# A hybrid attention and expert layer: TensorE's order written out from the first score to the routing, and w2 loaded with two consecutive rows on a partition

## The chip, the cores and the metric

The kernel runs on one core of one Trainium2 chip. A core has a matmul engine (TensorE, PE in the rows; PEld is its loading of weights), VectorE (DVE), ScalarE (ACT), GpSimd (POOL) and SyncE (SP, which here only issues transfers), an on-chip memory of 128 partitions (SBUF) and accumulators for TensorE (PSUM). Each engine works through its own list of instructions in order, and semaphores tie the lists together. The metric is the device time of the whole program in microseconds (us).

## What is computed

One layer over 512 latent tokens of width 1024 and 256 context tokens, all values fp32. The latent rows form a grid of 8 x 64. The parts that the change touches are the attention, the routing and the experts:

```python
h = modulate(rmsnorm(x, norm1_g), sh1, sc1)
q, k, v, hy_in, cf_in = split(h @ w_in)                  # 8 heads of 64 for q, k, v
attn = neighbourhood_attention(q, k, v, k_ctx, v_ctx)    # 8 x 16 window, and all context keys, one softmax
x = x + g1 * (concat(attn, hyena(hy_in), conformer(cf_in)) @ w_out)
h2 = modulate(rmsnorm(x, norm2_g), sh2, sc2)
aff = softmax(h2 @ w_router)                             # 16 experts
gate, idx = top_k(aff.T, 64)                             # every expert takes its 64 best tokens
xe = h2[idx]
y = (silu(xe @ w1) * (xe @ w3)) @ w2                     # w1, w3: 16 x 1024 x 2048, w2: 16 x 2048 x 1024
x = x + g2 * scatter_add(y * gate)
return rmsnorm(x, final_norm_g)
```

The expert weights are 16 x 24 MB and are each read once.

## The kernel before, in words

**Stages.** The Hyena filters, the modulation, the projections and the Hyena and conformer groups come first (0 to some 265 us of the profile), then the attention with the output projection and the routing (to 418 us), then the 16 experts, two by two, and the final norm.

**Attention.** The work is 16 pairs of heads and token blocks: hp counts four pairs of heads, b four blocks of 128 tokens. `scores(hp, b)` (L924) makes, for the two heads of a pair, a score tile of 128 tokens by 512 keys (256 of the window, 256 of the context): one matmul for each head (L932), on the upper and the lower 64 rows of TensorE. Then for each head DVE adds the bias and takes the minimum (L940; scores are negated), ACT takes the exponential and its sum (L943), DVE the reciprocal and the product (L944, L945). `ptrans` (L949) turns a tile of probabilities with four 128 x 128 transposes into a PSUM buffer of the tag T, of which there are two, and copies it to SBUF, by turns on ACT and DVE (L103, L105). `av` (L957) multiplies the turned probabilities by the values, 8 matmuls of 64 columns (L963), and splits the result on ACT and DVE into a high and a low part.

**Work beside it.** `out_part` (L902) multiplies the Hyena and conformer groups by their half of w_out: 12 matmuls for each of four blocks and two halves n (three products of high and low parts, L548 to L550), then DVE and POOL add to x. `out_proj(n, b)` (L1006) does the same with the attention's half. `x_rows` (L1019) transposes rows of x for the router (L1022, the same two PSUM buffers), `route(b)` (L1026) makes the router's logits and softmax in four pieces (L1044, L1050, L1063). `adaln(3)` is the last part of the modulation (L423, L431).

**Who sets the order.** Every engine's instructions are put in order by a list scheduler that takes those with the best priority whose operands it reckons ready; the priorities follow the source. Inside `tc.manual_schedule(engines={PE})` the source alone sets the order of TensorE's instructions. Before, that holds for an early stage and for the experts, and not for the attention, whose source is the generator `attention()` (L970) with 13 steps called in a row and then a list of words (L1114 to L1137): p for out_proj, l for the first half of x_rows, r for the next piece of a route, q for a quarter of an out_proj, a for the next attention step, f for its end.

**Loads.** 22 buffers of 1 MB (U) hold weights. `load` (L157 on) puts loads into a fixed list; SP issues them (L162) as buffers become free (`free`, `free_only`, `pump`), at most 22 at a time. The experts' loads are the end of the list: per expert 16 of w1 and w3 (128 rows of 2048 columns, one row of 8 KB on a partition) and 8 of w2 (256 rows of 1024 columns, L265 to L267; the partition p gets the rows p and p + 128, 4 KB each).

**Experts.** For each pair of experts a gather (L1162 on) builds the tokens' rows from one-hot matrices (L1170 on DVE) with 128 x 128 matmuls (L1178), copied and modulated by DVE and ACT (L1072, L1070). Each expert multiplies them by w1 and w3 into four PSUM tiles pa (L1290, L1291), copies these to SBUF as au (four tiles, 64 rows of w1's product above 64 of w3's), turns each with four transposes (L1317; the piece of au is the weights of the matmul, ident the moving operand), applies silu and the product (L1319, L1320) into hT, and multiplies hT by w2 (L1330). The result is scattered back with one-hot matmuls (L1188) and DVE adds (L1191) during the next expert's products.

Of the kernel before, what the change touches and what calls it, by code (L numbers as in the profile page):

```python
# [19 lines left out]
S = 512  # L20
# [30 lines left out]
def hybrid_kernel(ctx: ExitStack, tc: tile.TileContext, a, out: bass.AP):  # L51
    nc = tc.nc
# [23 lines left out]
    def free(k=1, keep=0):  # L76
        used[0] -= k
        pump(keep)

    def free_only(k=1):  # L80
        used[0] -= k
# [30 lines left out]
    ident = c1[:, C1["id"]]  # L112
# [46 lines left out]
    def load(key, src, view=lambda t: t):  # L159
        def go():  # L160
            t = U("ld")
            nc.sync.dma_start(view(t), src)  # L162
            ready[key] = t
        loads.append(go)
# [96 lines left out]
    for e in range(E):  # L261
        for k in range(8):
            load(("w1", e, k), a["w1"][e, k * 128:(k + 1) * 128, :])
            load(("w3", e, k), a["w3"][e, k * 128:(k + 1) * 128, :])
        for j in range(8):  # L265
            load(("w2", e, j), a["w2"][e, j * 256:(j + 1) * 256].rearrange("(k p) n -> p k n", p=128),
                 lambda t: t.rearrange("p (k n) -> p k n", n=1024))  # L267


    def norm_rows(rows, junk, n, ss, name):  # L270
# [499 lines left out]
    def finish(*gens):  # L770
        for g in gens:
            for _ in g:
                pass
# [79 lines left out]
    parts = []  # L853
# [49 lines left out]
    def out_part(n):  # L903

        for b in range(4):
            ps = psA("pX")
            for k in range(4):
                mm3(ps, [v512(m[1])[:, k, 128 * b:128 * b + 128] for m in (mixh, mixl)],
                    [w[:, k] for w in wov[n, 1]], k == 0, k == 3)
                yield  # L910
            s = slice(n * 512, (n + 1) * 512)
            t = W("t")
            nc.vector.tensor_mul(t, ps, g1bc[:, s])
            nc.gpsimd.tensor_add(xblk(b)[:, s], xblk(b)[:, s], t)
# [52 lines left out]
        nc.scalar.activation(h, ps[:, 0:128], AF.Copy)  # L967
        nc.vector.tensor_sub(v512(mixl[0])[:, hp, c], ps[:, 0:128], h.bitcast(FT))

    def attention():  # L970
        ps = deque()
        steps = [(hp, b) for hp in range(2) for b in range(4)] + [(hp, b) for b in range(4) for hp in (2, 3)]
        parts = [out_part(0), out_part(1)]
        build_tm(1)
        fetch_bias(2)
        for i in range(len(steps) + 1):
            if i < len(steps):
                ps.append(scores(*steps[i]))
            for _ in range(4):
                if i < 4:  # L980
                    next(parts[0])
                elif 5 <= i < 9:
                    next(parts[1])
            if i == 8:
                finish(parts[1])
                free_only(4)
            if i >= 1:
                hp, b = steps[i - 1]
                av(b, hp, [ptrans(p) for p in ps.popleft()])
                if b == 3:  # L990

                    free((1, 2, 1, 3)[hp], PK[hp])
                    if hp < 2:
                        build_tm(hp + 2)
                    if hp == 0:
                        fetch_bias(3)
                    if hp == 1:
                        load_wo(0, 0, 2)
                        load_wo(1, 0, PK[4])
            if i == 3:  # L1000
                finish(parts[0])
                free_only(2)
                load_wo(1, 1, PK[5])
            yield

    def out_proj(n, b):  # L1006
        ps = psA("pX")
# [91 lines left out]

    xr = [take(("xr", 0)), take(("xr", 1))]  # L1100
    limit[0] = 99
    att = attention()
    ada3 = adaln(3)
    for i in range(13):
        next(att)
        if i >= 10:
            next(ada3)

    def steps(g, at):

        for i, _ in enumerate(g):
            for other in at.get(i, ()):
                next(other, None)

    def one(f, *args):
        f(*args)
        yield

    PE = {mybir.EngineType.PE}
    rt = [route(b) for b in range(4)]  # L1120
    left = lambda b: one(x_rows, b, 0)
    go = lambda *g: [next(i, None) for i in g]
    op = {(n, b): out_proj(n, b) for n in range(2) for b in range(4)}
    for w in "p00 l0 p10 a r0 a p11 p01 r0 l1 r1 r0 r1 a p02 p12 q13 r1 r2 q13 r1 r0 q03 l2 q03 a f p13 r2 p03 r2 l3 r3 r3 r2 r3 r3".split():
        if w == "a":
            go(att)
        elif w == "f":
            finish(att)
            free(2, 0)
        elif w[0] == "p":  # L1130
            finish(op[int(w[1]), int(w[2])])
        elif w[0] == "q":
            go(op[int(w[1]), int(w[2])])
        elif w[0] == "l":
            go(left(int(w[1])))
        elif w[0] == "r":
            go(rt[int(w[1])])  # L1137

    free(6, 0)
    finish(ada3)  # L1140
# [137 lines left out]
    for e in range(E):  # L1278
# [35 lines left out]
        for f in range(4):  # L1314
            p = psT("pT")
            for i in range(4):
                nc.tensor.transpose(p[:, i * 128:(i + 1) * 128], au[f][:, i * 128:(i + 1) * 128], ident)  # L1317
            pv = p.rearrange("p (i a n) -> p i a n", i=4, a=2)
            nc.scalar.activation(hT[:, 4 * f:4 * f + 4], pv[:, :, 0], AF.Silu)  # L1319
            nc.vector.tensor_mul(hT[:, 4 * f:4 * f + 4], hT[:, 4 * f:4 * f + 4], pv[:, :, 1])  # L1320
# [132 lines left out]
```

## Time and profile before

| what | value |
|---|---|
| median of 3 runs | 1370.36 us (1369.19 to 1371.82) |
| the profiled execution | 1374.3 us |
| its span, first to last instruction | 1372.4 us |
| PE busy | 1267.0 us, 92% of the span |
| DVE, ACT, POOL busy | 491.7, 213.8, 154.4 us |
| read from and written to HBM | 453.87 and 2.36 MB, 332 GB/s over the span |
| mean granted clock of TensorE | 0.955 |
| w1 and w3 matmuls (L1290, L1291) | 1024 each, 455.5 and 455.8 us |
| w2 matmuls (L1330) | 1024, 223.5 us |

The page of the profile lists each engine's busy time, cuts the span into 40 slices, and follows the chain that ended last back from the last instruction: at each step to what released it. The waits are told from semaphores: an engine was idle until an instruction of another engine or a transfer ended. A timeline row gives the start and the time of a run of like instructions on one engine. [...] The rows themselves stand below.

### The profile page before, as it was taken

The page shows a single profiled execution, that of the slowest core. Times are in us where ns is not written, and L with a number is a line of the kernel's source. Part 1 is how long each engine was busy: PE and PEld are TensorE (multiplying, and loading weights), DVE is VectorE, ACT ScalarE, POOL GpSimd, SP SyncE. Part 2 cuts the span into 40 slices and gives each one's busy share as a digit, 9 for nine tenths or more (in the row PEclk, how much of TensorE's full clock was granted, in tenths as well). Part 3 has the DMA queues.
Part 4 walks back from the last instruction along what each step waited for, and adds up shares of the span by engine and source line. Part 5 has one row for each costly group of instructions (what it writes and reads, how often), then busy time and mean ns, then how long its engine had stood idle before and what let it go on. Part 6 is the DMA issues. An engine that isn't in the chain of part 4 may idle for free.

```text
span 1372.4 us, 15073 instructions
## 1 busy us (share of the span) xinstructions
PE 1267.0 (92%) x6084; PEld 614.1 (45%) x6084; DVE 491.7 (36%) x971; ACT 213.8 (16%) x445; POOL 154.4 (11%) x166
## 2 busy tenths in 40 slices
PE   5998989899979999998998999899899989989997
PEld 2576567765644334335334433433533343344332
DVE  6777998577471121212112121221212112111224
ACT  3532232245330100001000000000000000000002
POOL 1333433546110000000000000000000000000000
PEclk9999999999999999998997999999799999979999
DMA  9934124624466997999999999999999999999995
GB/s 353 350 128 174 67 66 112 222 83 154 151 264 264 419 416 320 417 416 419 414 421 414 419 416 416 418 414 422 414 420 415 417 418 414 421 414 421 413 418 216
DMA packets 89364, 458.01 MB, mean 334 GB/s; under 512 B 7364, under 2 KB 9228, under 8 KB 54478
## 3 DMA queue, kind: packets, MB, share of 16 engines
q1 hardware_dynamic: 88046, 453.64, 82.4%
q0 software_dynamic: 912, 3.06, 0.9%
q8 instruction: 48, 0.79, 0.2%
q10 hardware_dynamic: 336, 0.35, 0.1%
q14 instruction: 22, 0.18, 0.0%
HBM read 453.87 MB, written 2.36 MB: 332 GB/s over the span
## 4 chain that ended last, share of the span: by engine, by line
PE 69%; DVE 14%; DMA 13%; issue 2%; ACT 1%; POOLq 0%; DVEq 0%; SPq 0%; ACTq 0%
PE pa L1290 25%; PE py L1330 12%; DMA ld<-in_w_dram 11%; PE pT L1178 7%; DVE glu L590 4%; PE pZ L1188 4%; PE pT L1317 2%; PE pS L932 2%; PE pO L963 2%; PE pP L550 1%; PE pT L952 1%; PE pM L431 1%; PE pP L549 1%; PE pP L548 1%; PE pa L1291 1%
## 5 line engine op out<-in xcount | busy, mean ns | idle before, releaser
L1291 PE MATMUL pa<-ld,xh 128*64 128x512 f32 x1024 | 455.8, 596 | 5.5 <-DMA ld<-in_w_dram 5.5
L1290 PE MATMUL pa<-ld,xh 128*64 128x512 f32 x1024 | 455.5, 596 | 0.2 <-DVE xh L1072 0.2
L1290 PEld LDWEIGHTS pa<-ld,xh 128*64 128x64 f32 x1024 | 135.5, 137 | 271.8 <-issue 266.0
L1330 PE MATMUL py<-ld,xh 128*64 128x512 f32 x1024 | 223.5, 594 | 0.0
L1191 DVE TENSOR_TENSOR acc<-acc,pZ 128x512 f32<-128x512 f32 x112 | 72.0, 684 | 300.3 <-PE pZ L1188 300.3
L1291 PEld LDWEIGHTS pa<-ld,xh 128*64 128x64 f32 x1024 | 135.3, 137 | 32.1 <-issue 19.4
L1330 PEld LDWEIGHTS py<-ld,xh 128*64 128x64 f32 x1024 | 72.1, 137 | 140.3 <-issue 136.8
L1178 PE MATMUL pT<-ohg,ld 128*128 128x128 f32 x512 | 101.7, 363 | 31.4 <-DVE xh L1072 15.5
L103 ACT ACTIVATE au<-pa 128x512 f32<-128x512 f32 x32 | 19.1, 597 | 636.9 <-PE pa L1291 636.9
L1178 PEld LDWEIGHTS pT<-ohg,ld 128*128 128x128 f32 x512 | 87.6, 256 | 49.1 <-DVE xh L1072 22.4
L1357 POOL DMA_INDIRECT out_dram<-yg,where x1 | 1.1, 1116 | 952.9 <-DVE yg L1356 952.9
L1334 DVE SCALAR_TENSOR_TENSOR yg<-py,ig,g1bc 128x512 f32<-128x512 f32 x16 | 12.0, 752 | 205.1 <-PE py L1330 205.1
L516 POOL TENSOR_TENSOR wl<-ld,wh 128x512 fp32r<-128x512 f32 x44 | 63.8, 1478 | 90.1 <-ACT wh L515 54.3
L1188 PE MATMUL pZ<-yg,oh 64*128 64x512 f32 x240 | 68.9, 641 | 1.5 <-DVE acc L1191 1.5
L548 PE MATMUL pP<-hh,wh 128*128 128x512 f32 x144 | 59.2, 412 | 1.2 <-ACT hh L505 1.2
L550 PE MATMUL pP<-hh,wl 128*128 128x512 f32 x144 | 57.7, 409 | 2.7 <-DVE wl L516 2.7
L549 PE MATMUL pP<-hl,wh 128*128 128x512 f32 x144 | 57.7, 402 | 1.5 <-DVE hl L507 1.5
L590 DVE SCALAR_TENSOR_TENSOR glu<-glu,p 128x512 f32<-128x512 f32 x60 | 58.0, 967 | 1.1
L1317 PE MATMUL pT<-c,au 128*128 128x128 f32 x256 | 43.7, 305 | 11.9 <-DVE acc L1191 5.4
L1072 DVE TENSOR_SCALAR xh<-pT,A,B 128x128 f32<-128x128 f32 x32 | 13.1, 410 | 111.5 <-PE pT L1178 111.5
L105 DVE COPY au<-pa 128x512 f32<-128x512 f32 x32 | 22.1, 692 | 76.0 <-PE pa L1291 72.9
L1317 PEld LDWEIGHTS pT<-c,au 128*128 128x128 f32 x256 | 30.6, 153 | 29.4 <-DVE xh L1320 12.9
(336 smaller groups left out, 1303.5 us busy)
## 6 DMA issues: line engine op xcount, KB each, us to landing
ld<-in_w_dram SPq DMA_DIRECT2D x384, 1024.0 KB, 19.7
ld<-in_w_mod_dram SPq DMA_DIRECT2D x24, 1024.0 KB, 13.3
ld<-in_w_in_dram SPq DMA_DIRECT2D x11, 1024.0 KB, 5.2
ld<-in_w_out_dram SPq DMA_DIRECT2D x4, 1024.0 KB, 5.4
ld<-in_x_dram SPq DMA_DIRECT2D x2, 1024.0 KB, 11.5
ld<-in_x_dram SPq DMA_DIRECT2D x4, 512.0 KB, 6.8
out_dram<-acc SPq DMA_DIRECT2D x4, 512.0 KB, 6.2
g<-in_rpb_dram POOLq DMA_DIRECT2D x8, 244.5 KB, 3.9
```

The source lines that it names most:

```text
L516: (nc.vector if i in dve else nc.gpsimd).tensor_sub(lo[:, s], raw[:, s], hi[:, s].bitcast(FT))
L548: mm(ps, l[0], r[0], start=start, stop=False)
L549: mm(ps, l[0], r[1], start=False, stop=False)
L550: return mm(ps, l[1], r[0], start=False, stop=stop)
L590: nc.vector.scalar_tensor_tensor(yc[i], glt[i][:, j:j + 512], cw[:, i, j:j + 1], yc[i], op0=OP.mult, op1=OP.add)
L1178: mm(pk, xblk(b)[:, k * 128:(k + 1) * 128], g[:, b * 128:(b + 1) * 128], start=(b == 0), stop=(b == 3))
L1188: mm(ps[h], oh[pr, 128 * c:128 * c + 128], yg[pr], start=True, stop=True)
L1191: nc.vector.tensor_add(ablk(c)[:, s], (ablk if e else xblk)(c)[:, s], ps[h])
L1290: mm(pa[f][0:64], xT[:, k, cs], w1[:, s], start=(k == 0), stop=(k == 7))
L1291: mm(pa[f][64:128], xT[:, k, cs], w3[:, s], start=(k == 0), stop=(k == 7))
L1317: nc.tensor.transpose(p[:, i * 128:(i + 1) * 128], au[f][:, i * 128:(i + 1) * 128], ident)
L1330: mm(py[64 * h:64 * h + 64], hT[:, f], w2[:, i * 1024 + 512 * h:i * 1024 + 512 * h + 512], start=(f == 0), stop=(f == 15))
```

## The change

There are three edits. The generator and the word list are replaced by one string of words inside `tc.manual_schedule(engines={PE})`: S is a score pair, T the transposes of a pair's probabilities, A the value product, x a quarter of an out_part block, w and e the ends of the two out_parts, d a piece of the modulation, and p, l, r as before; q is gone. So TensorE's order in this stage is that of the source, and the other engines' is still the scheduler's. The loads of w2 put the rows 2p and 2p + 1 on the partition p, one run of 8 KB. For the block i of hT to have the rows p * 2 + k that the w2 tile now has, a transpose takes every second column of au, from `c = 256 * (i // 2) + i % 2`. Lines after the attention stand 10 or 11 lower (L1022 becomes L1012, L1317 becomes L1307).

```diff
@@ -263,8 +263,8 @@
             load(("w1", e, k), a["w1"][e, k * 128:(k + 1) * 128, :])
             load(("w3", e, k), a["w3"][e, k * 128:(k + 1) * 128, :])
         for j in range(8):
-            load(("w2", e, j), a["w2"][e, j * 256:(j + 1) * 256].rearrange("(k p) n -> p k n", p=128),
-                 lambda t: t.rearrange("p (k n) -> p k n", n=1024))
+
+            load(("w2", e, j), a["w2"][e, j * 256:(j + 1) * 256].rearrange("(p k) n -> p (k n)", k=2))
 
 
     def norm_rows(rows, junk, n, ss, name):
@@ -967,41 +967,31 @@
         nc.scalar.activation(h, ps[:, 0:128], AF.Copy)
         nc.vector.tensor_sub(v512(mixl[0])[:, hp, c], ps[:, 0:128], h.bitcast(FT))
 
-    def attention():
-        ps = deque()
-        steps = [(hp, b) for hp in range(2) for b in range(4)] + [(hp, b) for b in range(4) for hp in (2, 3)]
-        parts = [out_part(0), out_part(1)]
-        build_tm(1)
-        fetch_bias(2)
-        for i in range(len(steps) + 1):
-            if i < len(steps):
-                ps.append(scores(*steps[i]))
-            for _ in range(4):
-                if i < 4:
-                    next(parts[0])
-                elif 5 <= i < 9:
-                    next(parts[1])
-            if i == 8:
-                finish(parts[1])
-                free_only(4)
-            if i >= 1:
-                hp, b = steps[i - 1]
-                av(b, hp, [ptrans(p) for p in ps.popleft()])
-                if b == 3:
-
-                    free((1, 2, 1, 3)[hp], PK[hp])
-                    if hp < 2:
-                        build_tm(hp + 2)
-                    if hp == 0:
-                        fetch_bias(3)
-                    if hp == 1:
-                        load_wo(0, 0, 2)
-                        load_wo(1, 0, PK[4])
-            if i == 3:
-                finish(parts[0])
-                free_only(2)
-                load_wo(1, 1, PK[5])
-            yield
+
+    pairs_ = [(hp, b) for hp in range(2) for b in range(4)] + [(hp, b) for b in range(4) for hp in (2, 3)]
+    at_s, at_t, at_a = (iter(pairs_) for _ in range(3))
+    probs, turned = deque(), deque()
+
+    def score_step():
+        probs.append(scores(*next(at_s)))
+
+    def turn_step():
+        next(at_t)
+        turned.append([ptrans(p) for p in probs.popleft()])
+
+    def value_step():
+        hp, b = next(at_a)
+        av(b, hp, turned.popleft())
+        if b == 3:
+
+            free((1, 2, 1, 3)[hp], PK[hp])
+            if hp < 2:
+                build_tm(hp + 2)
+            if hp == 0:
+                fetch_bias(3)
+            if hp == 1:
+                load_wo(0, 0, 2)
+                load_wo(1, 0, PK[4])
 
     def out_proj(n, b):
         ps = psA("pX")
@@ -1099,42 +1089,41 @@
 
     xr = [take(("xr", 0)), take(("xr", 1))]
     limit[0] = 99
-    att = attention()
     ada3 = adaln(3)
-    for i in range(13):
-        next(att)
-        if i >= 10:
-            next(ada3)
-
-    def steps(g, at):
-
-        for i, _ in enumerate(g):
-            for other in at.get(i, ()):
-                next(other, None)
-
-    def one(f, *args):
-        f(*args)
-        yield
-
-    PE = {mybir.EngineType.PE}
+
     rt = [route(b) for b in range(4)]
-    left = lambda b: one(x_rows, b, 0)
-    go = lambda *g: [next(i, None) for i in g]
     op = {(n, b): out_proj(n, b) for n in range(2) for b in range(4)}
-    for w in "p00 l0 p10 a r0 a p11 p01 r0 l1 r1 r0 r1 a p02 p12 q13 r1 r2 q13 r1 r0 q03 l2 q03 a f p13 r2 p03 r2 l3 r3 r3 r2 r3 r3".split():
-        if w == "a":
-            go(att)
-        elif w == "f":
-            finish(att)
-            free(2, 0)
-        elif w[0] == "p":
-            finish(op[int(w[1]), int(w[2])])
-        elif w[0] == "q":
-            go(op[int(w[1]), int(w[2])])
-        elif w[0] == "l":
-            go(left(int(w[1])))
-        elif w[0] == "r":
-            go(rt[int(w[1])])
+    parts = [out_part(0), out_part(1)]
+    build_tm(1)
+    fetch_bias(2)
+
+    order = """S x0 x0 x0 x0 S T x0 x0 x0 x0 A S T x0 x0 x0 x0 A S T x0 x0 x0 x0 A w S T A d d
+               S T x1 x1 x1 x1 A S T x1 x1 x1 x1 A S T x1 x1 x1 x1 A S T x1 x1 x1 x1 e A S T d A S T d A
+               S T p00 A S T p10 A S T l0 p01 A S T r0 p11 A l1 S T r0 p02 r1 A r0 r1 p12 T l2 r0 r1 A f
+               r2 p03 r1 r2 p13 l3 r2 r3 r2 r3 r3 r3"""
+    with tc.manual_schedule(engines={E_.PE}):
+        for w in order.split():
+            if w in "STA":
+                {"S": score_step, "T": turn_step, "A": value_step}[w]()
+            elif w[0] == "x":
+                next(parts[int(w[1])])
+            elif w == "w":
+                finish(parts[0])
+                free_only(2)
+                load_wo(1, 1, PK[5])
+            elif w == "e":
+                finish(parts[1])
+                free_only(4)
+            elif w == "d":
+                next(ada3)
+            elif w == "f":
+                free(2, 0)
+            elif w[0] == "p":
+                finish(op[int(w[1]), int(w[2])])
+            elif w[0] == "l":
+                x_rows(int(w[1]), 0)
+            elif w[0] == "r":
+                next(rt[int(w[1])], None)
 
     free(6, 0)
     finish(ada3)
@@ -1314,7 +1303,8 @@
         for f in range(4):
             p = psT("pT")
             for i in range(4):
-                nc.tensor.transpose(p[:, i * 128:(i + 1) * 128], au[f][:, i * 128:(i + 1) * 128], ident)
+                c = 256 * (i // 2) + i % 2
+                nc.tensor.transpose(p[:, i * 128:(i + 1) * 128], au[f][:, c:c + 255:2], ident)
             pv = p.rearrange("p (i a n) -> p i a n", i=4, a=2)
             nc.scalar.activation(hT[:, 4 * f:4 * f + 4], pv[:, :, 0], AF.Silu)
             nc.vector.tensor_mul(hT[:, 4 * f:4 * f + 4], hT[:, 4 * f:4 * f + 4], pv[:, :, 1])
```

TensorE, attention, before: the end of an out_part block (pX), the value product of a pair (pO, from the values v, vodd and the context's vc) and the transposes of the next (pT, from c, the identity, and the probabilities P), and the next score pair (pS).

```order
L549 MATMUL pX<-wl,mixh_1174 128x512
L550 MATMUL pX<-wh,mixl_1175 128x512
L963 MATMUL pO<-PT,v 64x128
L952 MATMUL pT<-c_72,P 128x128 x3
L963 MATMUL pO<-PT,v 64x128 x3
L963 MATMUL pO<-PT,vodd 64x128 x2
L963 MATMUL pO<-PT,vc_1463 64x128 x2
L952 MATMUL pT<-c_72,P 128x128 x5
L932 MATMUL pS<-KK,Q 128x512 x2
L548 MATMUL pX<-wh,mixh_1174 128x512
```

The same place after the change:

```order
L549 MATMUL pX<-wl,mixh_1174 128x512
L550 MATMUL pX<-wh,mixl_1175 128x512
L963 MATMUL pO<-PT,v 64x128 x4
L963 MATMUL pO<-PT,vodd 64x128 x2
L963 MATMUL pO<-PT,vc_1463 64x128 x2
L932 MATMUL pS<-KK,Q 128x512 x2
L952 MATMUL pT<-c_72,P 128x128 x8
L548 MATMUL pX<-wh,mixh_1174 128x512
```

The transposes no longer stand between the value matmuls, and the score pair comes ahead of them.

TensorE, before, further on: scores beside the transposes of x for the router (L1022, ld is x) and out-projections (pX).

```order
L932 MATMUL pS<-KK,Q 128x512
L1022 MATMUL pT<-c_72,ld 128x128 x4
L932 MATMUL pS<-KK,Q 128x512
L963 MATMUL pO<-PT,vodd 64x128 x5
L963 MATMUL pO<-PT,vc_1463 64x128 x2
L952 MATMUL pT<-c_72,P 128x128 x4
L932 MATMUL pS<-KK,Q 128x512
L952 MATMUL pT<-c_72,P 128x128 x4
L932 MATMUL pS<-KK,Q 128x512
```

After, around the first transposes of x (now L1012):

```order
L963 MATMUL pO<-PT,vodd 64x128 x6
L963 MATMUL pO<-PT,vc_1463 64x128 x2
L932 MATMUL pS<-KK,Q 128x512 x2
L952 MATMUL pT<-c_72,P 128x128 x8
L1012 MATMUL pT<-c_72,ld 128x128 x4
L548 MATMUL pX<-wh,mixh_1909 128x512
L549 MATMUL pX<-wl,mixh_1909 128x512
```

Before, the score matmuls of this stretch stand alone; now they stand two by two, the transposes of a pair are eight in a row, and those of x follow directly.

SP's list at its end, before, with its last rows alternating between the two forms for 16 experts:

```order
L188 DMA ld<-in_x_dram 128x1x1024 x4
L162 DMA ld<-in_w_out_dram 128x4x512 x3
L162 DMA ld<-in_w_mod_dram 128x2x1024 x4
L162 DMA ld<-in_w_dram 128x2048 x16
L162 DMA ld<-in_w_dram 128x2x1024 x8
```

After, all 384 loads have one form:

```order
L188 DMA ld<-in_x_dram 128x1x1024 x4
L162 DMA ld<-in_w_out_dram 128x4x512 x3
L162 DMA ld<-in_w_mod_dram 128x2x1024 x4
L162 DMA ld<-in_w_dram 128x2048 x384
L1330 DMA out_dram<-acc_3527 16x8x1024 x2
```

Nothing changes its place on SP; the w2 loads have the shape of the others.

## Rows read from the trace of the kernel before

**Rows 1.** The page, part 4: the chain that ended last, share of the span by engine.

```profile
PE 69%; DVE 14%; DMA 13%; issue 2%; ACT 1%; POOLq 0%; DVEq 0%; SPq 0%; ACTq 0%
```

**Rows 2.** Waits of PE, 265 to 394 us (total, times, longest), and line L932.

```profile
PE pS L932 <- DVE KK L105: 4.3, 1, 4.3
...
L932 PE MATMUL pS<-KK,Q x64: 589/589/1216, 265.4 to 370.4; 64*128 64x512 f32 x64
```

**Rows 3.** Timeline of PE, 280 to 289 us (start, us, engine, line, operation).

```profile
280.51 1.03 PE L952 MATMUL pT<-c,P 128*128 128x128 f32 x8
281.48 1.13 PE L932 MATMUL pS<-KK,Q 64*128 64x512 f32 x4
282.54 0.50 PE L548 MATMUL pX<-wh,mixh 128*128 128x512 f32 x1
...
285.50 0.43 PE L963 MATMUL pO<-PT,v 128*64 128x128 f32 x2
...
288.05 1.13 PE L932 MATMUL pS<-KK,Q 64*128 64x512 f32 x4
```

**Rows 4.** The same timeline, 358 to 372 us.

```profile
358.45 1.12 PE L932 MATMUL pS<-KK,Q 64*128 64x512 f32 x2
359.50 0.66 PE L952 MATMUL pT<-c,P 128*128 128x128 f32 x4
...
370.90 0.88 PE L963 MATMUL pO<-PT,vodd 128*64 128x128 f32 x12
...
371.93 0.64 PE L1044 MATMUL pR<-xT,rwA 128*32 128x128 f32 x16
```

**Rows 5.** Timelines of DVE and ACT, 360 to 368 us.

```profile
360.80 0.68 DVE L940 CUSTOM_DVE_ANT_1 P<-pS,tm 128x512 f32<-128x512 f32 x1
...
365.41 0.71 ACT L943 ACTIVATE P<-P,m 128x512 f32<-128x512 f32 x1
...
366.95 0.59 ACT L103 ACTIVATE PT<-pT 128x512 f32<-128x512 f32 x1
```

**Rows 6.** Waits of SP's queue, 420 to 540 us.

```profile
SPq L162 <- PE py L1330: 44.8, 16, 21.6
```

**Rows 7.** SP's issues of w2 (862 to 871) and w1/w3 loads (872 to 903).

```profile
L162 SPq DMA_DIRECT2D ld<-in_w_dram x4: 327/328/328, 862.6 to 870.3; - x4
...
L162 SPq DMA_DIRECT2D ld<-in_w_dram x13: 327/328/3252, 872.8 to 902.6; - x13
```

**Rows 8.** Windows: us, busy per engine, PEclk, DMA share, GB/s.

```profile
870.20:910.10 39.90, 38.94 (x189) 14.17 (x190) 5.81 (x11) 1.97 (x5) 0.00 (x0) 1.00 1.01 419
...
1092.20:1112.70 20.50, 15.58 (x94) 10.56 (x94) 5.81 (x13) 3.39 (x7) 0.00 (x0) 1.00 1.03 413
1212.60:1233.10 20.50, 16.62 (x71) 11.76 (x71) 5.18 (x11) 2.57 (x5) 0.00 (x0) 0.71 1.03 413
```

**Rows 9.** Chain that ended last, 505 to 1260 us (start, us, what).

```profile
506.62 1.52 PE pT L1178 x8
...
623.04 1.77 PE pT L1178 x8
...
1095.93 1.11 PE pZ L1188 x4
...
1114.38 1.86 PE py L1330 x7
...
1192.78 19.86 DMA ld<-in_w_dram
...
1216.34 1.11 PE pZ L1188 x4
...
1219.09 1.46 PE pT L1178 x8
...
1241.54 13.99 PE py L1330 x64
```

**Rows 10.** Line L1317: ns min/median/max, first and last start.

```profile
L1317 PEld LDWEIGHTS pT<-c,au x256: 137/141/231, 454.8 to 1348.9; 128*128 128x128 f32 x128
```

## The prediction

> **What bounds the kernel now.** I read four views in this order: the chain that ended last, the waits of TensorE and of the SyncE queue, TensorE's timeline of the attention, and the chain of the last experts with the windows around it. The chain's shares [rows 1] put 69% of the span on PE, but a share is an average over stages, so I ask in each stage which wait ends last.
>
> In the attention stage (265 to 394 us) it is PE itself. The list of PE's waits there has one entry, 4.3 us at the second score, behind one DVE copy of the keys [rows 2]. Everything else is PE running instructions one behind the other, so this stage gets shorter only if PE gets less to do or does it in less time, and it gets longer if PE begins to wait.
>
> In the expert stage the weight stream decides up to 1212.6 us. SP waited for a buffer 16 times until a w2 product of an early expert freed one [rows 6]; after that the loads go out without a gap at a steady pace [rows 7], at 413 to 419 GB/s with a DMA share over 1 [rows 8]. The chain runs through these loads up to the one that lands at 1192.78 + 19.86 = 1212.6 [rows 9]. After it the chain has PE, DVE and ACT only: the rest of expert 13, the gather for the last two experts, and those two. The first experts still live on loads that came early and run at PE's pace: the gathers at 506.62 and 623.04 are 116.4 apart [rows 9]; then the stream catches up with them. So two savings add up. What the attention saves moves the first expert, the freeing of the buffers and with them the stream to the left by the same amount; and what each load saves in the stream comes off the landing at 1212.6.
>
> **Part 1, PE's order in the attention.** The arithmetic stays: 16 score pairs (S), 16 transposes of probabilities (T), 16 value products (A), the same out-projections and routing steps. What changes is how they are cut up.
>
> Scores: a pair is two matmuls on the two halves of the rows. Side by side the pair takes 282.54 - 281.48 = 1.06 us (its follower starts at 282.54; the pair's row is in [rows 3], its own 1.13 us contains the drain). A lone half takes 359.50 - 358.45 = 1.05 [rows 4], so a half costs what a pair costs. The 64 records of L932 [rows 2] would be 16 rounds if all were paired; PE's timeline has 22 rounds from 265.4 to 370.4, 6 too many: 6 x 1.05 = 6.3 us. The new order writes each pair's matmuls next to each other, and PE keeps source order.
>
> T and A: a whole T takes 281.48 - 280.51 = 0.97 [rows 3], a whole A 371.93 - 370.90 = 1.03 [rows 4], together 2.00. Where the scheduler put A's matmuls between the transposes, both take from 285.50 to 288.05, 2.55 [rows 3]: the switch between 64-column and 128-column work costs 0.55. Some 12 of 16 steps are cut in that way: 12 x 0.55 = 6.6 us. Together 12.9 us less on PE, and PE is the bound here.
>
> What source order adds are waits, because nothing may be pulled forward into them now. The rows for their price: the min-and-add on DVE takes 0.68, the exponential 0.71 on ACT, the copy of a transposed half 0.59 [rows 5]. In most steps T and A have a score pair, an out-projection of 2.96 us or another step ahead of them, and the copies fit under that. These places are without such cover. A directly behind T after the fourth block: copy 0.59 plus an exponential ahead of it on ACT, 1.3. Two later steps with only a piece of the modulation between T and A: 0.7 each, 1.4. The first l, the transposes of x placed directly behind T: they need one of two PSUM buffers, which is free when both min-and-adds, one exponential and one copy of this step are done, 2 x 0.68 + 0.71 + 0.59, less T's own 0.97: 1.7. The second l: 1.0, as an A stands in between. Three routing steps near the end, half a second of a microsecond each: 1.5. In all 6.9; behind each of them on PE stands the whole rest of the stage, so all of it counts. Net: 12.9 - 6.9 = **6.0 us**. Ends: all waits hidden, 12.9; waits as large as the gain, 0. The 4.3 us wait at the second score stays, since its copy is ordered on DVE, which the change leaves to the scheduler.
>
> The modulation's third piece, d, comes some steps earlier; its loads stand ahead of every expert's in SP's list, in both kernels. The tail from the last out-projection to the first expert matmul, a chain over DVE, ACT, POOL and PE, is not touched. 0 for both.
>
> **Part 2, the loads of w2.** 16 experts x 8 loads, each 1 MB. Before, a partition gets two runs of 4 KB from rows 128 apart; now one run of 8 KB, which is the form of the w1 and w3 loads. So the price after is in the trace: w1/w3 loads issue every (902.6 - 872.8)/12 = 2.483 us, w2 loads every (870.3 - 862.6)/3 = 2.567 [rows 7]. Per expert 8 x 0.084 = 0.67 us. By bandwidth: 8 x 1.0486 MB = 8.389 MB take 20.02 us at 419 and 20.31 at 413 GB/s [rows 8], 0.29 us. I take the middle, 0.5, since the issue pace is quantised by when earlier loads finish and the windows are blurred at their edges. The stream that decides holds the w2 of experts 2 to 12, 11 of them: 11 x 0.5 = **5.5 us** (ends 3.2 and 7.4). The later w2 loads are ahead of their use and count nothing.
>
> [...]
>
> **Part 3, the strided transposes.** To keep the rows of hT in the order of the new w2, each of the 16 transposes per expert reads every second column of au as its weights. The trace of before has no weight load with a step; the contiguous one takes 0.137 to 0.231, median 0.141 [rows 10]. Ends: 0, and a doubling, 0.14 more per transpose. I take 0, as the nearest row is the same instruction on the same tile, and it is loaded beside the matmul before. If that cover is gone, see the slower rival.
>
> [...]
>
> **Sum.** 1374.3 (the profiled execution) - 6.0 - 5.5 = 1362.8. The profiled execution lies 3.9 above the median of the three runs, 1370.36, so the median comes to 1370.36 - 11.5 = **1358.9 us**.
>
> **Rivals.**
>
> *The last gather runs at full clock.* After the last DMA wait, the gather and transposes from 1216.34 to 1241.54 take 25.2 us at a granted clock of 0.71; the same work from 1095.93 to 1114.38 takes 18.45 at 1.00 [rows 8, 9]. [...] For it: the gather before it has the full clock with the same instructions. Against: nothing in its own work or in what stands just ahead of it changes. 1358.9 - 6.75 = 1352.1.
>
> *The waits eat the order's gain.* If DVE and ACT are later than I counted at a few more steps, part 1 is 0: 1370.36 - 5.5 = 1364.9. [...]
>
> *w2's pace has another cause* (for instance that PE reads and frees differently in those stretches) and stays: 1370.36 - 6.0 = 1364.4. Against it: the two paces go with the form of the load, by distance and by bandwidth [rows 7, 8].
>
> *Both vanish*, because the effects are smaller and cancel: 1370.
>
> *Slower: the strided weight load is twice as long.* Per expert 16 x 0.141 = 2.26 us more on PE, as a transpose waits for its weights. A pair of experts then takes 116.4 + 4.5 = 120.9, and from the gather at 506.62 - 6.0 the seventh comes at 500.6 + 6 x 120.9 = 1226.0 instead of 1219.09, where the stream no longer decides; the three experts after it add 6.8. 6.9 + 6.8 = 13.7 slower, 1384.1. It decides from the point where 500.6 + 6 x (116.4 + 2c) - 1219.1 + 3c is above 0, c = 1.3 us per expert or 0.08 per transpose; below that the stream hides most of it.
>
> **Numbers.** My forecast 0.42; last gather at full clock 0.20; waits eat the order 0.14; w2 stays 0.08; both vanish 0.07; strided load slower 0.09. This kernel's runs can tell about 0.2%, 2.7 us, from no change. Faster by more than that: 0.42 + 0.20 + 0.14 + 0.08 = 0.84; the same 0.07; slower 0.09. The range of 8 in 10 runs from 1350, the full-clock case with part 1 a little better, to 1367, the cases with one part lost and the other at its lower end; it leaves out the two last cases and the thin tails.
>
> **What would show it.** Scores in 16 rounds, T and A whole, and PE's waits between 265 and 394 at some 11 us in place of 4.3, with the first expert matmul some 6 us earlier: part 1. Issue distance of 2.48 us in all loads, and the last DMA-gated step near 1201 instead of 1212.6: part 2. L1307's weight loads at 0.14: part 3. It is wrong if PE's waits grow by 13 us or more, if the w2 stretches stay at 413 GB/s, or if the gathers of the later pairs come 121 us apart with no DMA wait between.

## The result

The changed kernel takes **1357.47 us** (median of 4 runs, 1351.04 to 1362.26), the kernel before 1371.09 beside it (4 runs, 1369.19 to 1372.43): 0.9899 of the time, 95% interval 0.9853 to 0.9944, so 1.0% faster. The forecast was 1358.9. The profiled execution took 1362.26 us, 12.0 less than that of before, with a span of 1360.5; it is the slowest of the four.

The page of the profile after: busy time of the engines, DMA packets, and the shares of the chain.

```profile
PE 1253.2 (92%) x6084; PEld 614.1 (45%) x6084; DVE 491.1 (36%) x971; ACT 213.1 (16%) x445; POOL 154.3 (11%) x166
...
DMA packets 72980, 458.01 MB, mean 337 GB/s; under 512 B 7364, under 2 KB 9228, under 8 KB 21710
...
PE 65%; DMA 16%; DVE 15%; issue 2%; ACT 2%; POOLq 0%; DVEq 0%; SPq 0%; ACTq 0%
```

PE's busy time falls by 13.8 us. The packets under 8 KB fall from 54478 to 21710, by 32768: 16 experts x 8 loads x 256 rows. The chain, [rows 1] before, has 16% DMA instead of 13%, because ten waits for loads lie on it instead of eight.

The waits of PE from the first score to the last out-projection (in all, times, longest), which answer to [rows 2]:

```profile
PE pS L932 <- DVE KK L105: 4.1, 1, 4.1
PE pT L1012 <- ACT PT L103: 2.4, 3, 1.1
PE pO L963 <- ACT PT L103: 1.2, 1, 1.2
PE pR L1034 <- DVE lg L1042: 0.4, 1, 0.4
PE pO L963 <- DVE g1bc L1055: 0.3, 1, 0.3
PE pT L952 <- DVE P L945: 0.2, 1, 0.2
```

There are 8.6 us of waits where 4.3 stood, and the stage is shorter nevertheless, since PE has less to do. Windows over the whole stage (length, busy time and instructions of PE, PEld, DVE, ACT, POOL, then the granted clock as a share of full speed, the DMA share and GB/s), after and then before:

```profile
264.00:383.10 119.10, 110.23 (x761) 74.84 (x761) 83.40 (x203) 51.91 (x135) 51.59 (x75) 0.97 0.46 170
```

```profile
265.30:392.70 127.40, 123.01 (x761) 78.22 (x760) 84.16 (x205) 52.23 (x135) 52.42 (x75) 0.97 0.40 144
```

123.01 us of matmuls became 110.23, 12.8 less, for the same 761. The 64 score records stand in 16 rounds instead of 22, and every T and every A is in one piece. The steps, from PE's timeline, answer to [rows 3, 4]:

```profile
281.27 1.13 PE L932 MATMUL pS<-KK,Q 64*128 64x512 f32 x4
282.33 1.09 PE L952 MATMUL pT<-c,P 128*128 128x128 f32 x8
283.18 0.48 PE L548 MATMUL pX<-wh,mixh 128*128 128x512 f32 x1
...
286.11 0.88 PE L963 MATMUL pO<-PT,vodd 128*64 128x128 f32 x12
286.81 0.39 PE L963 MATMUL pO<-PT,vc 128*64 128x128 f32 x4
287.13 1.13 PE L932 MATMUL pS<-KK,Q 64*128 64x512 f32 x4
```

A pair of scores takes 1.06 us, T is one piece of eight, A one piece of sixteen; from one pair to the next it takes 5.86 us, where 281.48 to 288.05 was 6.57 before.

Windows in which the 16 loads of w1 and w3 and the 8 of w2 of one expert land, and over the last gather, as in [rows 8]:

```profile
799.40:839.10 39.70, 39.43 (x184) 13.56 (x183) 5.40 (x10) 1.43 (x4) 0.00 (x0) 1.00 1.01 421
839.10:859.00 19.90, 17.16 (x81) 10.22 (x78) 6.05 (x12) 2.11 (x4) 0.00 (x0) 0.82 1.01 420
1200.10:1229.10 29.00, 24.41 (x104) 18.58 (x104) 6.66 (x15) 4.18 (x9) 0.00 (x0) 0.65 1.01 422
```

w2 now moves at 420 GB/s in 19.9 us, like the others. The chain at the last transfer that PE waits for, as in [rows 9]:

```profile
1180.13 19.93 DMA ld<-in_w_dram
1200.06 0.04 issue
...
1229.13 6.15 PE py L1320 x27
```

That load lands at 1200.06 instead of 1212.6. Here is the whole way, cut at the same marks in each trace (us). The last column is the rest of the span. The last gather, in the windows and from here on, is the stretch of the last column but one: from that landing to expert 13's w2 product, with expert 13's remaining products of w1 and w3 in it.

| | first score to last out-projection | from there to the first expert matmul | to expert 1's w2 product | to the landing that gates expert 13 | to expert 13's w2 product | to the end |
|---|---|---|---|---|---|---|
| before | 127.35 | 25.16 | 107.61 | 687.13 | 28.82 | 130.9 |
| after | 119.10 | 24.39 | 110.65 | 681.89 | 29.00 | 131.4 |
| difference | -8.25 | -0.77 | +3.04 | -5.24 | +0.18 | +0.5 |

With the first score 1.37 us earlier (265.40 and 264.03, ahead of anything changed, and different in each execution) these add up to 11.9, the difference of the spans. The first column is the steadiest: 118.44 to 119.10 in the five executions with the string of the change (the change, e1, e7, e8, e11), 127.35 to 127.55 in the four with the old order (before, e2, e3, e4).

### The profile page after: what moved, and what is told of

Read it like the earlier page. It is cut to its first block, busy times and chain, and to the rows that moved or that the text cites. A ratio compares the mean times of both kernels' runs of the same rounds, so it can differ in the third digit from the quotient of the medians.

```text
span 1360.5 us, 15095 instructions
## 1 busy us (share of the span) xinstructions
PE 1253.2 (92%) x6084; PEld 614.1 (45%) x6084; DVE 491.1 (36%) x971; ACT 213.1 (16%) x445; POOL 154.3 (11%) x166
## 2 busy tenths in 40 slices
DMA packets 72980, 458.01 MB, mean 337 GB/s; under 512 B 7364, under 2 KB 9228, under 8 KB 21710
## 4 chain that ended last, share of the span: by engine, by line
PE 65%; DMA 16%; DVE 15%; issue 2%; ACT 2%; POOLq 0%; DVEq 0%; SPq 0%; ACTq 0%
PE pa L1279 24%; DMA ld<-in_w_dram 15%; PE py L1320 12%; PE pT L1167 7%; DVE glu L590 4%; PE pZ L1177 4%; PE pT L1307 2%; PE pP L550 1%; PE pP L548 1%; PE pP L549 1%; PE pS L932 1%; PE pO L963 1%; PE pM L431 1%; PE pX L548 1%; PE pX L550 1%
## 5 line engine op out<-in xcount | busy, mean ns | idle before, releaser
L1280 PEld LDWEIGHTS pa<-ld,xh 128*64 128x64 f32 x1024 | 135.6, 137 | 20.4 <-issue 12.9
L103 ACT ACTIVATE au<-pa 128x512 f32<-128x512 f32 x32 | 19.1, 597 | 632.3 <-PE pa L1280 632.3
L1307 PE MATMUL pT<-c,au 128*128 128x128 f32 x256 | 46.0, 315 | 11.4 <-DVE acc L1180 5.4
L1307 PEld LDWEIGHTS pT<-c,au 128*128 128x128 f32 x256 | 36.9, 209 | 25.7 <-DVE acc L1180 11.2
```

Source lines behind the costliest of these rows:

```text
L1280: mm(pa[f][64:128], xT[:, k, cs], w3[:, s], start=(k == 0), stop=(k == 7))
L1307: nc.tensor.transpose(p[:, i * 128:(i + 1) * 128], au[f][:, c:c + 255:2], ident)
```

## The experiments

All marks below are cut as in that table.

**One part alone.** e1 has the new order with the old loads and transposes, e2 the old order with the new loads and transposes.

```diff
 e1 = after, with
-a["w2"][e, j * 256:(j + 1) * 256].rearrange("(p k) n -> p (k n)", k=2)
+a["w2"][e, j * 256:(j + 1) * 256].rearrange("(k p) n -> p k n", p=128)
-au[f][:, c:c + 255:2]
+au[f][:, i * 128:(i + 1) * 128]
 e2 = before, with the same lines the other way round
```

> The changed order of TensorE in the attention, with the old loads of w2 (rows p and p + 128) and the old transposes. Theory (the two savings add): the last out-projection ends 8 us earlier from the first score, as in the changed kernel; up to 3 us of it are lost again before the second expert's w2 product, because the clock there differs; the stream keeps its 20.4 us for the 8 loads of w2 and the last DMA-gated step comes 5 to 8 us earlier. Total 1363 to 1366 us. Rival (the stream alone was worth something, the order is hidden behind it): within 2 us of the kernel before, 1369 to 1372.

> The old order, with the new loads of w2 and the strided transposes. Theory: the start of the expert stage does not move; 8 loads of w2 take 19.85 us instead of 20.4, 11 experts, so the last DMA-gated step comes 5 to 6 us earlier; the strided weight loads take 0.21 us instead of 0.14 and cost 0.2 to 0.3 us per expert after the stream. Total 1365 to 1367. Rival (w2's pace has another cause): DMA-gated step unmoved, 1370 to 1372.

e1: 1364.92 us, 0.9948 (0.9929 to 0.9967). e2: 1364.08 us, 0.9943 (0.9925 to 0.9961). The product of the two ratios is 0.989, that of the change 0.990, so the parts add, as far as these intervals tell. Each has its own stage: in e1 the attention is 118.44 us and the stream 687.05, in e2 127.55 and 681.29. Windows of e1 over w1/w3 and w2 loads and the last gather, then of e2 over w2 loads and the last gather:

```profile
864.00:903.80 39.80, 38.84 (x189) 14.39 (x189) 5.81 (x11) 1.97 (x5) 0.00 (x0) 1.00 1.01 420
903.80:924.20 20.40, 19.31 (x94) 6.91 (x92) 5.64 (x10) 2.73 (x6) 0.00 (x0) 1.00 1.03 412
1206.80:1228.50 21.70, 16.95 (x104) 11.43 (x104) 6.71 (x15) 4.15 (x9) 0.00 (x0) 1.00 1.03 414
```

```profile
905.20:925.10 19.90, 18.86 (x90) 7.23 (x88) 5.98 (x11) 2.73 (x6) 0.00 (x0) 1.00 1.02 421
1205.10:1230.70 25.60, 20.95 (x104) 15.35 (x104) 6.74 (x15) 4.18 (x9) 0.00 (x0) 0.80 1.01 421
```

The last gather shows that the cut of the table matters: it has 21.7 us at a granted clock of 1.00 in e1 and 25.6 at 0.80 in e2. e1's early gather does not come out whole at the end: its rest takes 134.1 us instead of 131, as PE meets the stream again in expert 15. Both rivals fall. e2 is 0.9 us below the range expected for it.

**The two halves of the w2 edit.** e3 has only the new loads, e4 only the strided transposes, both on the kernel before.

```diff
 e3 = before, with
-a["w2"][e, j * 256:(j + 1) * 256].rearrange("(k p) n -> p k n", p=128)
+a["w2"][e, j * 256:(j + 1) * 256].rearrange("(p k) n -> p (k n)", k=2)
 e4 = before, with
-au[f][:, i * 128:(i + 1) * 128]
+au[f][:, c:c + 255:2]
```

> The old order and the old, contiguous transposes with the new loads of w2, so that the rows of w2 do not match those of hT: the experts' products are of permuted rows, the amount of work is the same. Theory: as with the strided transposes but without their price, 0.5 to 1 us faster than e2, 1364 to 1366. Rival (the stride hides completely): same as e2 to within 0.3 us in every stage.

> The old order and the old loads with the strided transposes, so that the rows of hT do not match those of w2: permuted rows, the same work. Theory: LDWEIGHTS of the transposes 0.209 instead of 0.141, the time from the last product to the first w2 matmul grows by 0.2 to 0.3 us per expert, hidden by the stream up to the last DMA-gated step; after it 3 experts, so 0.5 to 1 us slower, 1371 to 1372. Rival (each of the 16 transposes pays 0.068): 1.1 us per expert, 3.3 us slower, 1374 or more.

e3: 1364.59 us, 0.9952 (0.9935 to 0.9969); e4: 1372.65 us, 1.0007 (0.9994 to 1.002). The loads make the gain, the stride costs nothing that the total shows; e3 was expected 0.5 to 1 us below e2's 1364.08 and isn't. But the weight loads of the transposes are longer in e4 (ns min, median, max):

```profile
L1318 PEld LDWEIGHTS pT<-c,au x256: 194/209/231, 454.3 to 1350.7; 128*128 128x128 f32 x128
```

From expert 13's w2 product to the end of expert 15's it takes 121.66 us before, 121.96 in e4; 121.56 in e3 and 121.95 in e2. That is 0.15 to 0.2 us per expert, not the 16 x 0.068 = 1.1 of the rival: most of the longer load costs no time. The profile after has eight of these loads from 445.45 to 446.49 us and their eight matmuls from 445.45 to 446.68, so they run side by side there; before it was 454.78 to 455.64 and 454.79 to 455.88.

**The price of a cut on PE.** e5 tears every score pair apart, e6 puts A into the next T again.

```diff
 e5 = after; scores() gets a hook, called between the two score matmuls
+            if s == 0:
+                between()
 e6 = after; av() gets a hook behind its first matmul; in the string, 10 times
-A S T
+B S
```

In e5 the hook makes the four transposes of the waiting pair's first half. In e6 B is one value matmul, three transposes of the next pair, the other seven value matmuls and the other five transposes.

> The changed kernel, with the transposes of a pair's first half put between the two score matmuls in 15 of the 16 steps. Theory (a lone half costs what a pair costs): 15 x 1.05 = 15.8 us more on TensorE between the first score and the last out-projection, less up to 3 us because some of the waits there shrink: that stretch grows from 119 to 132 to 135 us. Rival (the six lone halves of the kernel before cost little, and the stage got shorter for another reason): it grows by under 5 us.

> The changed kernel, with the value product of a step cut into the next step's transposes (1 value matmul pair, 3 transposes, 7, 5) in 10 steps, as the kernel before had it, and the score pair behind them. Theory (a cut costs 0.55 us): 10 x 0.55 = 5.5 us more between the first score and the last out-projection; waits may differ by 1 us. Rival (the cut is free, 2.55 us was the sum of other things): within 1 us of the changed kernel's 119 us.

There is one run of each, e5 1376.78 us and e6 1365.04, with 1371.24 for the kernel before. e5: the stage takes 133.39 us, 14.3 more, inside the expected 132 to 135. The window over the stage and a step of the timeline:

```profile
263.50:396.90 133.40, 127.74 (x761) 78.58 (x761) 84.53 (x203) 53.41 (x135) 51.24 (x75) 0.96 0.41 152
```

```profile
283.17 1.12 PE L932 MATMUL pS<-KK,Q 64*128 64x512 f32 x2
284.22 0.66 PE L954 MATMUL pT<-c,P 128*128 128x128 f32 x4
284.81 1.12 PE L932 MATMUL pS<-KK,Q 64*128 64x512 f32 x2
285.86 0.66 PE L954 MATMUL pT<-c,P 128*128 128x128 f32 x4
```

284.22 - 283.17 = 1.05 for a lone half, again what a pair costs; PE's busy time grew by 127.74 - 110.23 = 17.5, 1.17 for each of the 15, and the waits shrank. e6: the stage takes 125.95 us, 6.85 more. Its window and three rows of PE's waits:

```profile
265.60:391.60 126.00, 114.98 (x761) 76.01 (x761) 84.97 (x202) 52.77 (x135) 50.76 (x75) 0.97 0.44 162
```

```profile
PE pX L548 <- DVE m L940: 2.5, 3, 0.9
PE pT L952 <- DVE m L944: 2.3, 2, 1.8
PE pO L969 <- ACT PT L103: 1.3, 1, 1.3
```

114.98 - 110.23 = 4.75 is the work of 10 cuts, 0.48 each where I had taken 0.55; the rest is waits, 10.9 in all instead of 8.6, more than the 1 us I had allowed.

So the order's gain is a price for cuts that PE pays at once, not a stall that went away. At the prices of e5 and e6 the old order's 6 extra rounds of scores and some 12 cuts come to 6 x 1.17 + 12 x 0.48 = 12.8 us, which is what PE's work lost.

**Why w2's loads were slower.** e7 keeps runs of 4 KB but puts the two rows of a partition 8 KB apart; e8 gives w1 and w3 the old form of w2.

```diff
 e7 = after, w2
+a["w2"].rearrange("e f n -> (e f) n")[q:q + 512].rearrange("(p k) n -> p k n", k=4)[:, 0:3:2]
 e8 = after, w1 and w3
+a[n][e].rearrange("r (h n) -> (r h) n", h=2)[k * 256:(k + 1) * 256].rearrange("(k p) n -> p k n", p=128)
```

> The changed kernel, with each partition's two rows of a w2 load 8 KB apart instead of next to each other: two runs of 4 KB again, but near each other (some rows of w2 are read twice and others not at all; the amount of work is the same). Theory (the size of the run sets the pace): 8 loads of w2 take 20.4 us again, as before the change. Rival (the distance of 512 KB between the two rows set it): 19.85 us, as after.

> The changed kernel, with w1 and w3 in the old form of w2: two runs of 4 KB, 512 KB apart, on a partition (the products then mix wrong rows; the amount of work is the same). Theory (0.53 us for every 8 loads in that form): 16 loads take 40.7 to 40.9 us instead of 39.7; over the 12 experts ahead of the last DMA-gated step 12 us, so 1369 to 1373 us in place of 1357 to 1362. Rival (the form does not matter for these loads): no change.

Windows of e7 over w1/w3 and w2, and of e8 over the same:

```profile
860.50:900.30 39.80, 38.96 (x174) 16.63 (x176) 5.72 (x11) 2.13 (x6) 0.00 (x0) 0.89 1.01 420
900.30:920.70 20.40, 19.35 (x92) 7.38 (x90) 5.73 (x11) 2.73 (x6) 0.00 (x0) 1.00 1.03 411
```

```profile
862.60:903.50 40.90, 40.71 (x190) 13.80 (x190) 6.26 (x12) 1.15 (x3) 0.00 (x0) 1.00 1.03 410
903.50:923.40 19.90, 18.86 (x92) 7.42 (x90) 4.78 (x9) 2.73 (x6) 0.00 (x0) 1.00 1.01 420
```

In e7 8 loads of w2 take 20.4 us as before the change, though the rows are near: with runs of 4 KB they take 20.4 us at both distances (8 and 512 KB), with runs of 8 KB 19.9. In e8 the 16 loads of w1 and w3 take 40.9 instead of 39.7 and w2 keeps 19.9; the way to the gating load grows from 681.89 to 693.0 us. One run each: e7 1361.76 us, e8 1370.18. In e7 the total hides the loss, since its first two experts took 107.5 us and not 110.65, and its last gather 25.7 and not 29.0.

**What is still in it.** e9 to e12 change the string of words or the experts' part. The strings of e9, e10 and e12 have one r3 less than the change: they leave out the last piece of the routing of the last 128 tokens (one transpose, L1053, and its copy). It lies behind the last out-projection, so the first column is not touched by it; the second is 23.22 us there instead of 24.39, and up to 1.2 us of each total is this omission.

```diff
 e9 = after, in the string
-w S T A d d
+w S T d A d
-T l0 p01 A S T r0 p11 A l1 S T r0 p02 r1 A r0 r1 p12 T l2 r0 r1 A f
+T p01 l0 A S T p11 r0 A l1 S T p02 r0 r1 A r0 r1 T p12 l2 r0 r1 A f
 e10 = e9, with
-S x0 x0 x0 x0 S T x0 x0 x0 x0 A S T x0 x0 x0 x0 A S T x0 x0 x0 x0 A w
+S x0 x0 x0 x0 x0 x0 x0 x0 S T x0 x0 x0 A S T x0 x0 x0 A S T x0 x0 A w
 e11 = after, copies that sort the columns, and contiguous transposes
+copy(au[f].rearrange("p (j k m) -> p j m k", j=2, k=2), pa[f].rearrange("p (j m k) -> p j m k", j=2, k=2))
 e12 = e10, in gather()
-            if k % 4 == 0 or i == 0:
+            if True:
                 p = psT("pT")
```

> The changed kernel with another string of words: the first piece of the modulation before the fourth value product, and an out-projection block between a pair's transposes and the transposes of x that follow them, so that the copies from PSUM run beside it. Theory (these waits are on the path): TensorE's waits of 1.2, 1.1, 1.1, 0.3 and 0.3 us go, the stage from the first score to the last out-projection shrinks from 119.1 to 115.2 to 116 us, and the program by as much, 1353 to 1355 us beside 1357 to 1359 for the changed kernel. Rival (the stream or the tail takes it up): the stage shrinks and the total stays.

> As e9, and four more pieces of the Hyena and conformer groups' projection are put ahead of the second score, which waits 4.1 us for the keys' copy on DVE; the steps after it have fewer pieces. Theory: the wait shrinks by 2.9 us of work put into it, stage 112 to 113.5 us, total 1350 to 1352 us. Rival (the steps with three or two pieces lack cover, or DVE's copy comes later): stage no shorter than in e9.

> The changed kernel, with the columns of au put in order by the copies from PSUM (which then read PSUM with a step of 8 bytes), so that the transposes read contiguous columns. Theory: weight loads of the transposes 0.141 again, the two last experts 0.4 us shorter if the copies keep their 0.60 and 0.69 us. Rival (the strided PSUM read is slower): the copies grow by 0.1 us or more each and take back the 0.4.

> As e10, and the gathers take a new PSUM tile for each 128 columns of the model's width, so that a group of eight matmuls waits for the copy two groups back and not for the last one. Theory (after the last load that TensorE waits for, the gather and its clock decide): the time from that load's landing to expert 13's w2 product falls from 29 to 21 to 23 us; part of it is met again by the stream in expert 15, so the total falls by 3 to 6 us against e10, 1345 to 1348 us. Rival (the clock drops anyway and the copies are the bound): 27 us or more, total as e10.

e9: 1354.73 us (0.9852, 0.983 to 0.9874), the stage 114.44, 4.7 less than after and a little below the expected 115.2 to 116. The waits for the copies of L103 are gone. The rows that are left:

```profile
PE pS L932 <- DVE KK L105: 4.1, 1, 4.1
PE pR L1034 <- DVE lg L1042: 0.4, 1, 0.4
PE pO L963 <- DVE lg L1042: 0.4, 1, 0.4
PE pT L952 <- DVE P L945: 0.2, 1, 0.2
```

Its interval overlaps that of the change, so the total alone doesn't tell the two apart; the stage does. e10: 1350.68 us (0.9833, 0.9813 to 0.9853), as expected, but the stage is 113.76, only 0.7 better than e9, where 112 to 113.5 was expected. The wait did not shrink, it changed its place:

```profile
PE pX L548 <- DVE KK L105: 4.0, 1, 4.0
```

Now a block of the projection waits 4.0 us for the same copy of the keys, where the score did. A block needs no keys, but its accumulator comes from the same four PSUM buffers (tag A) as those of the scores and of the keys' projection that this copy empties. So it is the copy that counts: DVE does it at 271.87 us, behind four products for w_out (L867, 5.24 us in a row). No run moves that copy forward. The profiled execution is 6.1 us shorter than e9's, and not by the stage: the first two experts took 109.0 us here and 112.2 there, at a granted clock of 0.94 and 0.89, and the last gather 25.6 and 28.8, at 0.80 and 0.64.

e11: the weight loads are short again, and the copies grow by half and more (ns of the loads; for the copies busy us and mean ns). As the edit stands, they read PSUM in order and write each next element 512 bytes to and fro in SBUF, so it is the write that has the step, and not the read as expected:

```profile
L1306 PEld LDWEIGHTS pT<-c,au x256: 137/141/230, 443.5 to 1325.6; 128*128 128x128 f32 x128
...
L103 ACT ACTIVATE au<-pa 128x512 f32<-128x512 f32 x32 | 34.3, 1071 | 623.4 <-PE pa L1280 623.4
L105 DVE COPY au<-pa 128x512 f32<-128x512 f32 x32 | 34.1, 1065 | 69.8 <-PE pa L1280 67.9 <-PE pa L1279 1.9
```

597 became 1071 and 692 became 1065 ns; the last two experts take 121.96 us as with the stride. The median 1353.59 (0.9862, 0.9833 to 0.9891) is no proof of a gain, as the interval overlaps that of the change, and in the profiled execution the first two experts took 103.9 us instead of 110.65, at a granted clock of 1.00 instead of 0.92.

e12: 1340.85 us (0.9751, 0.9729 to 0.9773), the fastest of all, some 10 us below e10, where 3 to 6 had been expected. The last gather and what PE waits for in the experts:

```profile
1184.40:1203.10 18.70, 17.25 (x102) 13.07 (x102) 6.73 (x15) 4.18 (x9) 0.00 (x0) 0.91 1.01 422
...
PE pa L1280 <- DMA ld<-in_w_dram: 23.9, 25, 1.4
```

The last gather takes 18.7 us, 6.9 less than in e10 and less than the expected 21 to 23, and the first two experts, which hold a gather too, take 102.1 instead of 109.0. Some of this is given back: the last column grows by 5.3 us, as PE now waits 25 times for loads, 23.9 us in all, where after had 3.3; the last of these waits are in the last experts. No run shows this kernel with the last r3 in; by the second column it would be up to 1.2 us slower.

## Why the prediction was right, and where it wasn't

**Part 1 was said to give 6.0 and gave 8.25.** PE's work fell by 12.8 us; I had 12.9 from 6 extra rounds of scores and 12 cuts, and e5 and e6 confirm both prices (1.05 to 1.17, and 0.48 where I had 0.55). What failed in size is the term of the new waits, 4.5 instead of 6.9. The first A without cover waited 1.2 (I had 1.3), the two steps with d 0 (1.4), and the routing steps 0.4 and the A behind one of them 0.3 (1.5). The transposes of x waited 2.4 (2.7), but not where I had put it: 1.1 at the first l (I had 1.7), 0 at the second (1.0), and 1.1 and 0.2 at the first r0 and at l2, which also stand directly behind a T and which I had missed. The 4.3 us at the second score stayed, as 4.1.

**Part 2 was said to give 5.5 and gave 5.24** in the stream. From expert 1's w2 product to the landing it takes 687.01 to 687.13 us with the old loads (before, e1, e4) and 680.1 to 681.9 with the new (the change, e2, e5, e9 to e11), 5.1 to 7.0 less; in e3, e6 and e7 PE doesn't wait for that load. One reading was wrong, though not its number: counted in SP's list, the issues at 862.6 to 870.3 in [rows 7] are loads of w1 and w3 of expert 8, and those of 872.8 to 902.6 hold five of w2. A load lands 20 us after its issue, as the row of before for 862 to 871 says (min, median, max):

```profile
DMA to landing us min/median/max: 19.8/19.9/20.0
```

So the distance of 2.567 us is the pace at which the w2 loads issued earlier landed. The middle between pace and bandwidth, 0.5 us per expert, is what the marks show: 20.4 and 19.9, 2.5% less.

**Part 3 was wrong in its own row and right in the sum.** I took 0 because the nearest row was the same instruction. The load is half as long again:

```profile
L1307 PEld LDWEIGHTS pT<-c,au x256: 194/209/230, 445.4 to 1336.7; 128*128 128x128 f32 x128
```

The median went from 0.141 to 0.209 us, between the two ends, 0 and a doubling, of which the second was an estimate that no row of before showed. The stride costs 0.15 to 0.2 us per expert behind the stream (e4, e2), far below the 1.3 from which the slower rival would decide.

**What stood in no term.** Of the 8.25 + 0.77 us that the first expert gained, 3.04 were lost by the second expert's w2 product, 2.8 of them up to the end of expert 0's. Three windows from the first expert matmul to there, the last of them over expert 0's w2 product, after and then before:

```profile
407.50:429.50 22.00, 21.98 (x104) 9.11 (x104) 2.15 (x11) 0.91 (x2) 0.00 (x0) 0.92 0.65 247
429.50:450.10 20.60, 18.82 (x100) 9.01 (x98) 2.89 (x6) 4.44 (x8) 0.00 (x0) 0.97 1.01 422
450.10:465.00 14.90, 14.90 (x67) 4.84 (x68) 0.50 (x2) 0.38 (x1) 0.00 (x0) 0.92 1.01 422
```

```profile
417.90:440.00 22.10, 22.09 (x112) 9.74 (x112) 2.15 (x11) 0.92 (x2) 0.00 (x0) 0.97 0.69 270
440.00:458.80 18.80, 16.89 (x90) 7.42 (x89) 2.55 (x5) 4.37 (x8) 0.00 (x0) 1.00 1.01 424
458.80:472.60 13.80, 13.80 (x65) 4.65 (x66) 0.84 (x2) 0.45 (x2) 0.00 (x0) 1.00 1.02 424
```

PE waits 1.8 us in the three after and 1.9 in those before, but the granted clock is 0.92, 0.97 and 0.92 where it was 0.97, 1.00 and 1.00. The whole column goes with it: 103.9 us at a granted clock of 1.00 (e11), 107.6 at 0.95 (before), 109.0 at 0.94 (e10), 110.65 at 0.92 (the change), 112.35 at 0.89 (e1). Why the clock was lower stays open, and that the new order lowers it is not shown: the executions with the old order took 107.6 to 109.1, those with the string of the change and unchanged copies 107.5 to 112.4. So there was luck in the point forecast. In the profiled pair 2.3 more in part 1, 0.8 in the tail and 1.4 at the start, ahead of anything changed, met 3.0 less here. And the medians are 13.6 us apart, not the 11.9 of that pair, in runs of the change that spread over 11.2 us.

**The rivals.** "The last gather at full clock" isn't one case or the other: the gather took 29.0 us at 0.65 in the profile after, 25.6 at 0.80 in e2, 21.7 at 1.00 in e1. These are single executions of different kernels, so whether the kernel or the execution sets the clock is not shown. For the execution speaks that the mean granted clock of the four runs of the change is 0.952 to 0.966; only one of them was profiled, so the gather's share in their spread stays open. Its price is less than the 6.75 I gave: in e1 3 us came back in expert 15. "The waits eat the gain", "w2 stays" and the slower rival are refuted by e1, by e3 with e7 and e8, and by e4.

## What to carry to other kernels

Where one engine is busy without a gap, count how often its work is cut into pieces that cost more than their share: here half of a pair cost as much as the pair (1.05 and 1.06 us), and the 6 rounds saved were worth more than all the waits that a fixed order brought (6.3 to 7.0 us against 4.5). A price that the trace already holds for another instruction of the same form (here the loads of w1 and w3, 39.7 us for 16, with 19.9 for 8 of w2 after the change) can be taken over almost to the digit, while "the same instruction, with a stride" can not (0.209 us for 0.141). And cut a long run at marks (first score, first expert, last gated landing) before comparing totals, for a total hides the 5.24 us of a stream behind the 7.3 that lie between the last gather's 29.0 us at a granted clock of 0.65 and its 21.7 at 1.00.

## What was not expected of the hardware

- Weights with a step of 8 bytes took 0.209 us to load instead of 0.141, for 128 columns of fp32.
- Copies of 128 x 512 from PSUM that write neighbours 512 bytes apart took 1.071 us on ACT and 1.065 on DVE instead of 0.597 and 0.692.
- Eight loads with two rows of 4 KB on a partition took 20.4 us, and with one run of 8 KB 19.9, 2.5% less; with 8 KB and with 512 KB between the rows it was the same 20.4.
- The same last gather took 21.7, 25.6 or 29.0 us at a granted clock of 1.00, 0.80 or 0.65 (e1, e2, the change).
